# Constant matmuls in TensorE's gaps in the opening of a gated-attention trunk kernel

## Chip, cores and metric

The kernel runs on one core of one Trainium2 chip. The metric is the device time of one execution in microseconds (us). Three runs of the kernel before took 1215.12, 1215.80 and 1216.45 us; the median is 1215.8.

## What is computed

One layer over x, 1024 tokens by 1024 channels, all in float32. Cut to what matters:

```
mod = silu(c) @ ada_w + ada_b
shift, scale, gate = split(mod, 3)
h = rms_norm(x, norm_w) * (1 + scale) + shift
proj = h @ w_in
hq, hf, hi, hz, gq, gk, gv, gz, ga, mg = split(proj)
y_h = hgrn2_branch(hq, hf, hi, hz, lb, hgrn_norm_w)       # gated linear recurrence, 8 heads
y_g = gla_branch(gq, gk, gv, gz, ga, alpha_w, alpha_b, gla_norm_w)   # the same, 4 heads
merged = sigmoid(mg0) * (y_h @ w_branch[0]) + sigmoid(mg1) * (y_g @ w_branch[1])
x = x + gate * (merged @ w_out)
out = rms_norm(x, final_norm_w)
```

The change lies in the opening, where `h` is made and its first products with `w_in` (the columns of `gq` and `gk`) are formed.

## The kernel before

A large product is done as three float32r products: each operand is split into a high part (a cast on ScalarE, line 196) and a low part (a subtraction on VectorE, line 197), and high by high, high by low and low by high are summed in PSUM (`product`, line 350). Smaller products are plain float32 matmuls, each of which TensorE runs as two instructions.

The opening works on the first 512 tokens ("half" 0), four tiles of 128 tokens each, and on channels in blocks of 128. Its steps, in the order in which they are written:

- **Loads.** `load_x` (line 138) brings four tiles of x, `load_mod` (line 243) the columns of `ada_w` for shift and scale of one block of channels, `load_wg` (line 310) rows of `w_in`. All are issued by SyncE (SP), in the order of lines 143 to 144 and 360 to 367; later ones behind line 419.
- **Token norm.** `square_x` (ScalarE, line 200) and `scale_x` (VectorE, line 207) normalise one tile of x. `vec_rows` (line 152) turns a few rows of parameters into columns by a TensorE transposition; the one at line 371 handles `ada_b` and `norm_w`.
- **Transposition.** `turn_x` (line 214) transposes one block of 128 channels of the four tiles on TensorE into PSUM, line 219; `copy_x` (line 223) copies the result to SBUF on ScalarE. `transpose_x` (line 226) does both.
- **Modulation of one block.** `blocks` (line 240) lists five blocks of one or two times 128 channels. The contraction over 1024 has eight parts: `add_mod` (line 259) sums four of them on VectorE, `mm_mod` (line 271) does the other four by matmuls at line 277 with 32 columns each, and `end_mod` (line 280) adds the two (line 283), sums over the partitions by matmuls against a column of ones (line 287) and forms shift and scale (lines 290 and 292).
- **h and its products.** `make_h` (line 230) applies scale and shift on ScalarE (line 233) and splits the result. `products` (line 355) does one, two or three of the three parts of the product for all six accumulators: four in `acc0` (tiles `pd`) and two in `sc_ps`. `sc_ps` is a PSUM tile of 128x1024 that is first written by these products; its second half, columns 512 to 1023, is the sixth accumulator.

For the first block the order is: transposition of channel block 0, `add_mod(0)`, `mm_mod(0)`, `end_mod(0)`, `prep_wg(0)`. Then in the loop at line 378, with `bi` 0: `make_h`, preparation of two blocks of weights, `add_mod(1)`, transpositions of the next two blocks, the first part of the products, `mm_mod(1)`, the second part, `end_mod(1)`, the third part.

The order of the work on TensorE, ScalarE and VectorE is the written one from line 159 (`manual_schedule`) to line 446 (`order.close()`). Outside of it, and for SyncE and GpSimd throughout, the program's builder orders the instructions by when it reckons them ready and by the order in which they are written. Behind line 446 follow the rest of the products, the scans of the two branches, and the merging and output products (lines 541, 1343 and 1520 on TensorE).

`ones` (line 118) and `ident` (line 116) are constant 128x128 float32 tiles in SBUF, all ones and the identity, made by GpSimd at the start.

## Time and profile before

| | before |
|---|---|
| median of three runs | 1215.8 us |
| the profiled execution's own time | 1216.46 us |
| its span, first to last instruction | 1214.8 us |
| TensorE busy (matmuls) | 1184.1 us, 97% of the span |
| VectorE busy | 790.9 us, 65% |
| ScalarE busy | 546.9 us, 45% |
| GpSimd busy | 123.8 us, 10% |
| moved by DMA | 183.51 MB, 151 GB/s on average |

In the rows of the profile PE is TensorE's matmul side, PEld its weight loads, DVE is VectorE, ACT is ScalarE, POOL is GpSimd and SP is SyncE; SPq is SP's queue, from which transfers are issued. `L219` is line 219 of the kernel. In a row of the timeline the first number is the start in us from the beginning of the span, the second the duration, and `x4` says that four instructions of one kind were merged into the row; in brackets stands how long the engine had been idle and what ended it. The strip of 40 digits on the page gives the busy tenths in 40 equal slices of the span, about 30 us each. PEclk is the clock that was granted to TensorE.

### The profile page before, as it was taken

How to read it: one execution, taken by the hardware profiler on the slowest of the kernel's cores; microseconds unless marked ns; L12 is line 12 of the kernel's file. 1: busy time of each engine (PE TensorE's matmuls, PEld its weight loads, DVE VectorE, ACT ScalarE, POOL GpSimd, SP SyncE). 2: the span in 40 equal slices, each digit the busy share in tenths (PEclk: the TensorE clock that was granted, in tenths of full speed). 3: DMA queues.
4: the chain of work that ended last, by engine and by line, in shares of the span. 5: the costliest groups of instructions: out<-in, count | busy, mean ns of one | idle time of the engine just before them, and what ended most of it. 6: DMA issues, size and time to landing. Idle time of an engine off the chain costs nothing.

```text
span 1214.8 us, 20860 instructions
## 1 busy us (share of the span) xinstructions
PE 1184.1 (97%) x8579; PEld 982.6 (81%) x8579; DVE 790.9 (65%) x1245; ACT 546.9 (45%) x797; POOL 123.8 (10%) x215
## 2 busy tenths in 40 slices
PE   5999999999999999999999999999999999999997
PEld 3777889889798888888887888877778888878886
DVE  4637444774848456877884365794653775988994
ACT  5646732434434244344332324455743544444554
POOL 4100000202111121121110101011220000000000
PEclk9999999999999999999999999999999999999999
DMA  9814000844444267255341112054697746435523
GB/s 320 277 70 139 18 19 19 293 141 161 156 152 149 66 207 249 94 179 169 108 174 47 59 53 70 36 174 158 227 343 277 260 160 208 135 104 173 174 104 122
DMA packets 130961, 183.51 MB, mean 151 GB/s; under 512 B 7467, under 2 KB 97633, under 8 KB 130866
## 3 DMA queue, kind: packets, MB, share of 16 engines
q1 hardware_dynamic: 117250, 136.87, 35.7%
q0 software_dynamic: 13568, 45.31, 9.6%
q8 instruction: 67, 1.10, 0.4%
q14 instruction: 28, 0.23, 0.1%
q10 hardware_dynamic: 48, 0.01, 0.0%
HBM read 132.87 MB, written 49.28 MB: 150 GB/s over the span
## 4 chain that ended last, share of the span: by engine, by line
PE 61%; issue 23%; DVE 3%; ACT 3%; POOL 2%; DMA 1%; POOLq 0%; ACTq 0%; DVEq 0%
PE pd L541 19%; PE pd L1343 9%; PE sc_ps L1343 5%; PE pm L1343 5%; PE pd L1520 3%; PE pd L643 2%; PE pd L644 2%; PE pd L645 2%; PE sc_ps L1520 2%; PE pm L848 1%; PE pd L352 1%; PE pm L829 1%; PE pm L850 1%; PE pm L1520 1%; PE sc_ps L352 1%
## 5 line engine op out<-in xcount | busy, mean ns | idle before, releaser
L541 PE MATMUL pd<-b,b 128*128 128x512 f32 x1632 | 387.4, 394 | 0.0
L541 PEld LDWEIGHTS pd<-b,b 128*128 128x128 f32 x1632 | 302.4, 188 | 64.8 <-issue 1.4
L1343 PE MATMUL pd<-b,b 128*128 128x512 f32 x720 | 173.7, 392 | 4.3 <-ACT b L1414 2.1
L1343 PEld LDWEIGHTS pd<-b,b 128*128 128x128 f32 x720 | 133.7, 188 | 35.7 <-ACT b L1414 3.2
L197 DVE TENSOR_TENSOR b<-b,b 128x1024 fp32r<-128x1024 f32 (+2 forms) x89 | 98.9, 1122 | 83.1 <-ACT b L196 65.4
L196 ACT CAST b<-b 128x1024 fp32r<-128x1024 f32 (+2 forms) x89 | 82.9, 948 | 92.1 <-DVE b L1199 14.6
L1286 DVE TENSOR_TENSOR b<-b,b 128x1024 fp32r<-128x1024 f32 x56 | 68.3, 1224 | 66.9 <-ACT b L1285 52.3
L1285 ACT CAST b<-b 128x1024 fp32r<-128x1024 f32 x56 | 58.3, 1050 | 73.9 <-PE pd L1343 20.6
L1343 PE MATMUL sc_ps<-b,b 128*128 128x512 f32 x324 | 79.4, 391 | 1.0 <-ACT scT L793 1.0
L600 PE MATMUL pd<-b,b 128*128 128x256 f32 x256 | 74.2, 290 | 0.0
L1264 DVE TENSOR_TENSOR b<-b,b 128x1024 fp32r<-128x1024 f32 x48 | 59.2, 1251 | 20.8 <-ACT b L1263 15.1
L602 PE MATMUL pd<-b,b 128*128 128x256 f32 x256 | 72.5, 283 | 0.0
L601 PE MATMUL pd<-b,b 128*128 128x256 f32 x256 | 72.4, 283 | 0.0
L1343 PEld LDWEIGHTS sc_ps<-b,b 128*128 128x128 f32 x324 | 60.3, 188 | 14.6 <-ACT scT L793 1.4
L1343 PE MATMUL pm<-b,b 128*128 128x512 f32 x300 | 72.1, 389 | 0.0
L1263 ACT CAST b<-b 128x1024 fp32r<-128x1024 f32 x48 | 49.9, 1050 | 41.2 <-PE pd L1343 16.0
L1343 PEld LDWEIGHTS pm<-b,b 128*128 128x128 f32 x300 | 56.3, 188 | 11.7
L352 PE MATMUL pd<-b,b 128*128 128x512 f32 x192 | 53.3, 410 | 2.0 <-ACT b L196 0.9
L1201 POOL DMA_DIRECT2D ws<-b x64 | 34.6, 541 | 192.0 <-DVE b L1195 86.5
L735 ACT COPY xb<-b 128x512 f32<-128x512 f32 x48 | 29.4, 620 | 49.4 <-PE sc_ps L715 26.7
L643 PE MATMUL pd<-b,b 128*128 128x512 f32 x128 | 51.3, 401 | 0.0
L644 PE MATMUL pd<-b,b 128*128 128x512 f32 x128 | 50.0, 390 | 0.0
(285 smaller groups left out, 1964.3 us busy)
## 6 DMA issues: line engine op xcount, KB each, us to landing
b<-in_w_in_dram SPq DMA_DIRECT2D x66, 512.0 KB, 4.2
ws<-b POOLq DMA_DIRECT2D x64, 256.0 KB, 3.3
b<-ws SPq DMA_DIRECT2D x32, 512.0 KB, 4.9
b<-in_x_dram SPq DMA_DIRECT2D x16, 512.0 KB, 5.7
b<-in_ada_w_dram SPq DMA_DIRECT2D x32, 256.0 KB, 6.9
b<-in_w_branch_dram SPq DMA_DIRECT2D x16, 512.0 KB, 4.4
b<-h SPq DMA_DIRECT2D x14, 512.0 KB, 4.3
wo<-b POOLq DMA_DIRECT2D x14, 512.0 KB, 5.7
```

Of the source, the lines that this page charges most:

```text
L196: nc.scalar.copy(hi, src)
L197: nc.vector.tensor_sub(lo, src, hi.bitcast(F32))
L352: nc.tensor.matmul(accs[f], wg(a, d, f), b[d][:, half * 512:half * 512 + 512], start=(d == 0 and n == 0), stop=(d == KT - 1 and n == 2))
L541: nc.tensor.matmul(ps[0:w, th * 512:(th + 1) * 512], a[:, k, 0:w], b[:, th * 512:(th + 1) * 512], start=(k == 0 and n == 0), stop=(k == KT ...
L600: nc.tensor.matmul(o, lh, hi[:, k % 4, :], start=(k == 0), stop=False)
L601: nc.tensor.matmul(o, lh, lo[:, k % 4, :], start=False, stop=False)
L602: nc.tensor.matmul(o, ll, hi[:, k % 4, :], start=False, stop=(k == KT - 1))
L643: nc.tensor.matmul(o, lh, hi[:, k % 2, :], start=(k == 0), stop=False)
L644: nc.tensor.matmul(o, lh, lo[:, k % 2, :], start=False, stop=False)
L1286: nc.vector.tensor_sub(lo, t, hi.bitcast(F32))
L1343: nc.tensor.matmul(o, a[:, sl], c, start=(p in (1, 5) and kt == 0 and n == 0), stop=(kt == 3 and n == 2), skip_group_check=True)
L1520: nc.tensor.matmul(o, a, b, start=(p in (1, 5) and kt == 0 and n == 0), stop=(kt == 3 and n == 2), skip_group_check=True)
```

## The change

Seventeen calls of a float32 matmul of 128x128 by 128x128 on the constant tiles `ones` and `ident` are added on TensorE; their result goes to columns 512 to 639 of `sc_ps` and is overwritten by the first product of the sixth accumulator. Three stand behind the transposition of the parameter rows, two, four, three and two behind the four transpositions of channel block 0, one behind `mm_mod(0)`, and two between the transpositions of the next blocks and the first products. Line 372's `transpose_x` is written out as its two steps.

```diff
+    def keep_busy(n):
+        for _ in range(n):
+            nc.tensor.matmul(sc_ps[:, 512:640], ones, ident, start=True, stop=True)
+
-    def turn_x(half, xs, d):
+    def turn_x(half, xs, d, gaps=(0, 0, 0, 0)):
         if d % 2 == 0:
             hT[half, d // 2] = S.get([2, 512])
         turned[half, d] = mtile()
         for i in range(4):
             nc.tensor.transpose(turned[half, d][:, i * P:(i + 1) * P], xs[i][:, d * P:(d + 1) * P], ident)
+            keep_busy(gaps[i])
...
     vec_rows(rows_a, 24, R_SH)
-    transpose_x(0, x_t, 0)
+    keep_busy(3)
+    turn_x(0, x_t, 0, (2, 4, 3, 2))
+    copy_x(0, 0)
     add_mod(0)
     mm_mod(0)
+    keep_busy(1)
     end_mod(0)
     prep_wg(0)
...
         if nd == 1:
             for d in nxt:
                 transpose_x(0, x_t, d)
+            keep_busy(2)
             products(d0, (0,))
             mm_mod(bi + 1)
             products(d0, (1,))
```

`if nd == 1` holds in the loop for `bi` 0 alone, since the loop is left before it for the last block.

## The prediction

> **What bounds the kernel now.** I read the page first, then busy time by stretches, then the order of time of the opening.

> ```profile
> span 1214.8 us, 20860 instructions
> ...
> PE   5999999999999999999999999999999999999997
> ...
> PEclk9999999999999999999999999999999999999999
> DMA  9814000844444267255341112054697746435523
> ```

> TensorE (PE) is full in every slice but the first and the last. So the kernel's length is the time at which the products begin, plus a nearly fixed queue of products. The stretches say this more exactly (us; busy time and count of PE, PEld, DVE, ACT, POOL; granted clock; DMA share; GB/s):

> ```profile
> 0.00:24.45 24.45, 11.17 (x40) 5.88 (x40) 13.18 (x30) 14.10 (x27) 14.41 (x56) 1.00 0.96 311
> 24.45:1207.00 1182.55, 1172.98 (x8541) 976.70 (x8539) 775.47 (x1212) 530.56 (x766) 109.41 (x159) 1.00 0.45 148
> ...
> 8.00:14.00 6.00, 1.42 (x3) 0.54 (x3) 3.35 (x9) 3.26 (x7) 5.76 (x22) 1.00 1.13 305
> 14.00:23.00 9.00, 7.71 (x30) 4.62 (x30) 6.41 (x15) 5.19 (x11) 1.30 (x5) 1.00 1.07 366
> 23.00:32.00 9.00, 8.53 (x46) 6.05 (x48) 4.28 (x8) 4.53 (x8) 0.59 (x1) 1.00 1.08 362
> ```

> From 24.45 to 1207 us PE is busy for 1172.98 of 1182.55 us. Only 9.57 us are open there, and the change edits nothing in them. In the opening PE is idle for more than half of the time, while the DMA engines are full (share 1.07 to 1.13). The stretch of the first 24 us is therefore where the change must win or lose, and DMA is the first suspect for its bound. In order of time (start, duration, line, count, idle before and what ended it):

> ```profile
> 3.08 0.27 PE L154 MATMUL pm<-ident,rows_a 24*128 24x24 f32 x1 [0.49 <-DMA rows_a<-in_norm_w_dram]
> 7.34 0.48 PE L219 MATMUL pm<-ident,b 128*128 128x128 f32 x1 [3.99 <-DVE b L210]
> 8.69 0.47 PE L219 MATMUL pm<-ident,b 128*128 128x128 f32 x1 [0.88 <-DVE b L210]
> 11.43 0.47 PE L219 MATMUL pm<-ident,b 128*128 128x128 f32 x1 [2.27 <-DVE b L210]
> 13.11 0.47 PE L219 MATMUL pm<-ident,b 128*128 128x128 f32 x1 [1.21 <-DVE b L210]
> 14.47 1.08 PE L277 MATMUL pm<-b,cs 128*32 128x256 f32 x8 [0.88 <-DVE scT L267]
> 16.17 0.99 PE L287 MATMUL pm<-ones,scT 128*128 128x1 f32 x4 [0.62 <-DVE scT L283]
> 17.02 1.95 PE L219 MATMUL pm<-ident,b 128*128 128x128 f32 x8
> 19.17 2.07 PE L352 MATMUL pd<-b,b 128*128 128x512 f32 x4 [0.20 <-ACT b L196]
> 21.04 1.05 PE L352 MATMUL sc_ps<-b,b 128*128 128x512 f32 x2
> 22.02 1.05 PE L277 MATMUL pm<-b,cs 128*32 128x512 f32 x4
> 23.47 1.05 PE L277 MATMUL pm<-b,cs 128*32 128x512 f32 x4 [0.39 <-DMA b<-in_ada_w_dram]
> 24.45 1.21 PE L352 MATMUL pd<-b,b 128*128 128x512 f32 x4
> ```

> Two things are to be seen. First, at 23.47 the second half of the second modulation step (mm_mod(1)) starts when its weights land, after 0.39 us of waiting. From there PE runs on without a gap into the products at 24.45. Second, PE runs at half speed up to 22.02 (the halves of mm_mod(1) on either side of the wait already take the same 1.05), as the same work later in the kernel shows:

> ```profile
> 28.92 1.20 PE L352 MATMUL pd<-b,b 128*128 128x512 f32 x4
> 29.95 0.62 PE L352 MATMUL sc_ps<-b,b 128*128 128x512 f32 x2
> 30.41 1.07 PE L352 MATMUL pd<-b,b 128*128 128x512 f32 x4
> ...
> 55.34 0.64 PE L277 MATMUL pm<-b,cs 128*32 128x256 f32 x8
> ...
> 58.77 0.50 PE L287 MATMUL pm<-ones,scT 128*128 128x1 f32 x4
> ...
> 63.33 1.04 PE L219 MATMUL pm<-ident,b 128*128 128x128 f32 x8
> ```

> Six products take 22.02 - 19.17 = 2.85 us at the start and 30.41 - 28.92 = 1.49 us later. Eight transpositions take 1.95 against 1.04 us. The clock row reads full in the slow stretch too, so there I trust the durations and not the clock row.

> **The change part by part.** It removes nothing, moves nothing and adds no wait or DMA. It adds 17 calls of a 128x128 float32 matmul on constant tiles.

> *Price of one.* The nearest row at full speed has the same shape:

> ```profile
> L829 PE MATMUL pm<-b,b 128*128 128x128 f32 x112 | 14.0, 277 | 0.4 <-ACT b L808 0.4
> ```

> A float32 matmul is two instructions (mm_mod(0) issues four calls and shows x8). That gives 2 x 14.0 / 112 = 0.25 us at full speed. At half speed the nearest row is the eight transpositions of the same shape, one instruction each: 2 x 1.95 / 8 = 0.49 us. I take 0.49 where the clock is not yet up, and 0.25 as the other end.

> *Where they lie, at 0.49.* The three after the transposition at 3.08 end at 3.35 + 1.47 = 4.82; the next work starts at 7.34, so they are hidden. The two after the first x transposition end at 7.82 + 0.98 = 8.80 against 8.69, 0.11 late, which is hidden since the fourth transposition sets what follows. The four end at 9.27 + 1.96 = 11.23 against 11.43: hidden. The three end at 11.90 + 1.47 = 13.37 against 13.11: the fourth transposition is 0.26 late. The next two then end at 13.84 + 0.98 = 14.82 against 14.47, so mm_mod(0) is 0.35 late. The one behind it ends 0.49 after mm_mod(0), within the 0.62 us in which PE waits for DVE: hidden. The last two follow the eight transpositions. With the 0.35 these end at 19.32, so the two end at 20.30 against 19.17, and the first products are 1.13 late. At 0.25 each, every group fits its gap; the last two fit because the eight transpositions, started 0.93 earlier (below), then end at 16.09 + 1.04 = 17.13.

> *What full speed saves, if it comes before mm_mod(0).* mm_mod(0) takes 0.64 for 1.08 (0.44 saved) and the four at L287 take 0.50 for 0.99 (0.49 saved). These two are on the chain to the first products: the sums from L287 give the scale, ACT then scales and casts, and PE starts:

> ```profile
> 17.65 0.82 ACT L233 ACTIVATE b<-b,modv,amul 128x512 f32<-128x512 f32 x1 [1.38 <-DVE amul L292]
> 18.50 0.62 ACT L196 CAST b<-b 128x512 fp32r<-128x512 f32 x1
> ```

> So the products start at 19.17 - 0.93 = 18.24. They take 1.49 for 2.85 and end at 19.73 for 22.02. That is 2.29 us won on PE.

> *Where the 2.29 us go.* The next instruction that cannot move is the second half of mm_mod(1). Its data come by the queue of SP, which issues it in this order:

> ```profile
> 11.40 6.31 SPq L251 DMA_DIRECT2D b<-in_ada_w_dram x8
> 18.10 1.09 SPq L315 DMA_DIRECT2D b<-in_w_in_dram  x2
> 19.60 6.14 SPq L251 DMA_DIRECT2D b<-in_ada_w_dram x8
> ```

> The eight transfers of block 1 are issued from 11.40 to 17.71 us into full DMA engines, each behind a landing of an earlier transfer, and none behind PE. A faster PE does not move them. PE then waits 0.39 + 2.29 = 2.68 us before 23.47 in place of 0.39. What is late next is the landing, and it was late before. The other branch to the same point is DVE:

> ```profile
> 24.58 0.69 DVE L283 TENSOR_TENSOR scT<-scT,pm 128x512 f32<-128x512 f32 x1
> 25.96 0.95 PE L287 MATMUL pm<-ones,scT 128*128 128x1 f32 x8
> ```

> DVE's sum at 24.58 needs the end of mm_mod(1) at 24.52, which stays. It ends at 25.27 and PE asks for it at 25.96, behind its products. So nothing after 23.47 is pulled forward.

> *Sum.* Gain 0, since the landing covers all of the 2.29 us. In the other direction, if the clock stays low throughout, the products end 1.13 us later, at 23.15. The first half of mm_mod(1) then takes 1.05 and ends at 24.20, against 23.47, so 0.7 us are lost. I take 0, since PE is occupied almost without a hole from 11 us on and reached full speed before after 19.17 to 22.02 of dense work. Bounds from this sum are 0 and +0.7 us on the profiled execution's 1216.46 us (span 1214.8 and 1.7 around it), which stands 0.66 above the median of 1215.8.

> [...] The clock row shows nothing of the switch, but the durations put it at 22.02. [...]

> **The rivals.**

> *The clock's moment varies between executions.* If the switch came after 23.47 in some of the runs before, these lost time on path. The rows bound it: the three runs spread from 1215.12 to 1216.45, 1.33 us, and median to lowest is 0.7. An early switch would bring all runs to the lowest: about 1215.1. Against it stands that the profiled execution had the switch in time and yet took 1216.46. [...]

> *The landing is not the bound.* Were the wait at 23.47 for something on PE's or DVE's side, the 2.29 us would come through: 1215.8 - 2.3 = 1213.5. For it: the wait is only 0.39 us, so without it PE's speed would decide at once. Against it: the row names the transfer, and the DMA engines are full.

> *The added matmuls stand in the way at half speed* (the change does not do what it says): 1215.8 + 0.7 = 1216.5, decided by whether the products after the last two start later than 19.17.

> *Slower: the order behind the opening is laid anew.* From line 446 on, the builder of the program, and not the source, orders the instructions of PE, ACT and DVE by its own reckoning of when each is ready. The added calls shift that reckoning. The place is the later stages, where PE waits now and then:

> ```profile
> PE pd L1343 <- ACT b L1414: 2.1, 2, 1.8
> PE pd L1343 <- DVE b L953: 1.5, 1, 1.5
> ```

> An order that repeats these three waits elsewhere costs 3.6 us: 1219.4. It decides from the first place after 65 us at which two instructions have changed places. For it: 9.57 us of gaps exist, so gaps can grow or shrink. Against it: all three engines follow PE, so a common shift leaves most orders alone. A luckier order could give as much back: 1212.2.

> **How the numbers follow.** Hidden behind the landing, 0.52: about 1215.5, the median less a share of the second case. The clock's moment, 0.13: 1215.1. The landing not the bound, 0.05: 1213.5. Added matmuls in the way, 0.10: 1216.5. New order, 0.20: 0.12 slower, 0.08 faster. What a measurement of this kernel can tell from no change is about 0.2%, 2.4 us; even the full 2.29 us stay just under it. Faster by more is the lucky order and most of the third case, where noise helps it over: 0.12. Slower by more is the new order and 0.04 out of the first case for something that these rows do not show: 0.16. Within: 0.72. The range takes in the bounds, the 1213.5 case, and goes most of the way to the two ends of the new order: 1212.8 to 1218.8. The likeliest case's own range is 1214.5 to 1216.8.

> **What would show it.** Right: six products in about 1.5 us from about 18.3, then a wait of 2 us or more for the transfer before mm_mod(1), and its second half still at about 23.4; equal times from there to the end. Wrong: the second half of mm_mod(1) clearly before 23.4 (landing not the bound); transpositions at 1.95 us for eight and products after 19.5 (in the way); an order on PE that differs after line 446 and gaps beyond 9.57 us (new order). A transfer landing at another time without the queue having changed would break the central step.

## The result, and the profile after

The changed kernel takes 1219.69 us (median of 8 runs, 1218.78 to 1221.96) against 1215.93 us for the kernel before in the same job (8 runs, 1214.74 to 1217.61). The medians differ by 3.8 us, 0.31%; the ratio worked out from all 16 runs is 1.0034 with a 95% interval of 1.0024 to 1.0043. The kernel is slower, where no change was forecast. One execution of e1 below, the one that was profiled, took 3040.09 us with all its products slow, and is left out of the figures.

The page of the profiled execution (1220.52 us by its own time) has, beside the lines shown of before:

```profile
span 1218.8 us, 20928 instructions
...
PE   7999999999999999999999999999999999999997
...
PEclk9999999999999999999999999999989999999999
...
q8 instruction: 67, 1.10, 0.4%
```

The first slice is busier, as the added matmuls make it. There are 68 more instructions. And the clock row has a dent in the thirtieth slice, 884 to 914 us, which the kernel before did not have. The same stretches as before (columns as there):

```profile
0.00:24.45 24.45, 15.49 (x74) 11.08 (x74) 13.22 (x30) 13.99 (x27) 14.55 (x56) 1.00 0.95 308
24.45:1207.00 1182.55, 1172.15 (x8525) 975.98 (x8524) 773.12 (x1204) 528.50 (x760) 109.37 (x159) 1.00 0.45 147
```

PE is as full behind the opening as it was, but gets through 16 matmuls fewer (x8525 for x8541). Where time is lost cannot be seen from busy time here: a matmul at half clock counts as busy for longer (12 products take 5.49 us in place of 3.02 in the rows further down). TensorE's timeline in the opening:

```profile
14.79 1.08 PE L282 MATMUL pm<-b,cs 128*32 128x256 f32 x8 [0.38 <-DMA b<-in_ada_w_dram]
15.80 0.71 PE L216 MATMUL sc_ps<-ident,ones 128*128 128x128 f32 x2
16.49 0.58 PE L292 MATMUL pm<-ones,scT 128*128 128x1 f32 x4
...
19.07 1.21 PE L357 MATMUL pd<-b,b 128*128 128x512 f32 x4 [0.63 <-ACT b L196]
20.12 0.62 PE L357 MATMUL sc_ps<-b,b 128*128 128x512 f32 x2
22.27 1.05 PE L282 MATMUL pm<-b,cs 128*32 128x512 f32 x4 [1.52 <-DMA b<-in_ada_w_dram]
23.77 1.05 PE L282 MATMUL pm<-b,cs 128*32 128x512 f32 x4 [0.44 <-DMA b<-in_ada_w_dram]
24.75 1.20 PE L357 MATMUL pd<-b,b 128*128 128x512 f32 x4
```

The clock record of this execution starts at 16.28 us; up to there the durations are those of half speed, behind it of full speed (before: 22.02). The six first products take 20.74 - 19.07 = 1.67 us for 2.85. Then PE waits 1.52 and 0.44 us for `ada_w`, and the products behind go on at 24.75, 0.30 later than before. So the opening gives nothing and loses little. The order of instructions, but for the added calls, is that of before on all five engines. I set the starts of the same PE instructions side by side: the changed kernel is 0.3 us late at 24.45, 0.7 from 313 on, 0.2 at 886 (it gains a little between 830 and 860), 1.3 at 893, 4.2 at 900 and 4.0 at the end.

Most of the loss thus lies in 7 us around 893, where the output product begins. First the kernel before (L1414 is the sigmoid of `put_gate1` on ScalarE, L1415 its store by GpSimd), then the kernel after, whose lines there are 9 higher:

```profile
887.31 0.54 POOL L1415 DMA_DIRECT2D gate<-b  x1 [3.01 <-ACT b L1414]
...
892.22 0.60 ACT L1414 ACTIVATE b<-pd 128x512 f32<-128x512 f32 x1 [0.76 <-DMA gate<-b]
...
892.87 3.02 PE L1343 MATMUL pd<-b,b 128*128 128x512 f32 x12 [1.82 <-ACT b L1414]
```

```profile
887.98 0.54 POOL L1424 DMA_DIRECT2D gate<-b  x1 [3.49 <-ACT b L1423]
...
893.49 0.60 ACT L1423 ACTIVATE b<-pd 128x512 f32<-128x512 f32 x1 [1.97 <-DMA gate<-b]
...
894.14 5.49 PE L1352 MATMUL pd<-b,b 128*128 128x512 f32 x12 [2.88 <-ACT b L1423]
```

Read from the last row back: PE wants the PSUM tile that the sigmoid empties; the sigmoid wants the SBUF buffer from which an earlier gate store is still being read; that store was issued at 887.98. From its issue to the sigmoid 5.51 us pass, against 4.91 before. PE waits 2.88 us instead of 1.82: 0.60 of the 1.06 more is this longer store; the rest is that the store was issued 0.67 later, for a reason not followed up, while PE itself came 0.22 later. Then the same 12 products take 5.49 us instead of 3.02. The windows on either side of 893.50 say why:

```profile
890.09:893.50 3.41, 1.17 (x6) 0.63 (x4) 3.12 (x3) 1.44 (x4) 1.61 (x3) 1.00 1.05 398
893.50:900.33 6.83, 6.19 (x15) 4.84 (x16) 0.02 (x1) 1.68 (x3) 0.54 (x1) 0.50 1.00 367
```

The granted clock is 0.50 from 893.50 for 6.83 us. And the store takes longer, it seems, because of a transfer that no line of the source issues. The DMA view over that place, before (887 to 894 us) and after (887 to 895); columns are packets, MB and share of 16 engines:

```profile
q0 software_dynamic: 497, 1.78, 62.6%
q1 hardware_dynamic: 1416, 0.85, 42.9%
```

```profile
q0 software_dynamic: 567, 2.00, 63.0%
q1 hardware_dynamic: 1517, 1.11, 41.9%
q8 instruction: 1, 0.02, 0.9%
```

Queue q8 brought instructions, 67 times 16,384 bytes in an execution of the kernel before. Its page counts 17,158 instructions of TensorE (8579 on PE and as many on PEld), 256 to each of the 67; so I take q8 for TensorE's, an estimate that the runs below bear out. 0.9% of 16 engines over 8 us is 1.15 us of one engine. By the start times of its packets in the trace, a fetch came before at 863.4 and the next at 897.4 us; after, at 859.2 and 890.8, into the store that the boundary waits for. In f4, 256 added instructions brought one fetch more (68 for 67) and put the later ones back to about where they were (863.0 and 895.8 us).

### The profile page after: what moved, and what is told of

It reads as the page before. It is cut to its first block, busy times and chain, and to the rows that moved or that the text cites. A ratio compares the mean times of both kernels' runs of the same rounds, so it can differ in the third digit from the quotient of the medians.

```text
span 1218.8 us, 20928 instructions
## 1 busy us (share of the span) xinstructions
PE 1191.5 (98%) x8613; PEld 989.9 (81%) x8613; DVE 790.8 (65%) x1245; ACT 547.2 (45%) x797; POOL 123.9 (10%) x215
## 4 chain that ended last, share of the span: by engine, by line
PE 64%; issue 19%; DVE 5%; POOL 3%; DMA 2%; ACT 2%; POOLq 0%; ACTq 0%; DVEq 0%
PE pd L550 18%; PE pd L1352 10%; PE sc_ps L1352 5%; PE pm L1352 5%; PE pd L1529 3%; PE pd L652 2%; PE pd L654 2%; PE pd L653 2%; PE pd L611 2%; PE pd L610 2%; PE pd L609 2%; PE sc_ps L1529 2%; PE pm L857 1%; PE pm L838 1%; PE pd L357 1%
## 5 line engine op out<-in xcount | busy, mean ns | idle before, releaser
L196 ACT CAST b<-b 128x1024 fp32r<-128x1024 f32 (+2 forms) x89 | 83.0, 948 | 92.9 <-DVE b L1208 14.4
L1295 DVE TENSOR_TENSOR b<-b,b 128x1024 fp32r<-128x1024 f32 x56 | 68.3, 1224 | 71.3 <-ACT b L1294 49.3
```

The source lines that it names most:

```text
L196: nc.scalar.copy(hi, src)
L1295: nc.vector.tensor_sub(lo, t, hi.bitcast(F32))
```

## The experiments

The theories: **F**, the 68 added instructions shift every later instruction fetch, some now fall into transfers that are awaited, and a longer wait can drop the clock; **A**, each added instruction costs its issue; **H**, the faster opening leaves a hole in front of `mm_mod(1)`, and the clock pays for it; **W**, the early rise of the clock shifts the steps of 3.41 us at which the clock changes, which gives the fall at 893 (in the profile after, 893.50 is 877.22 us, 257 steps of 3.413, behind the rise at 16.28; in f1 to f4 the letter stands for another rival, named there); **N**, chance in when transfers land. That the order was laid anew was out already, since no two instructions had changed places. In e1, e3, e7, e8, e9, f2 and f4 small matmuls are put into the kernel before, one call of which is four instructions of TensorE (two matmuls and two weight loads); what they write is overwritten. They stand in the idle time behind the `vec_rows` call of line 371, so that the clock comes up as late as in the kernel before (21.6 to 23.4 us in the profiles, 19.7 in e3).

```diff
+    def tiny(n):
+        for j in range(n):
+            p0 = j % 4 * 32
+            nc.tensor.matmul(sc_ps[p0:p0 + 32, 512:513], ones[:, 0:32], ident[:, 0:1], start=True, stop=True)
...
     vec_rows(rows_a, 24, R_SH)
+    tiny(17)
```

The number is 17 in e1, e7 and f2 (68 instructions), 32 in e3 (128), 48 in e9 (192), 64 in e8 and f4 (256). e2 and f3 are the changed kernel with `keep_busy(3)` replaced by `tiny(50)`: the early clock, with 256 instructions added. All times are medians in us; each job has its own runs of the kernel before. The ratios are worked out from the runs of both kernels and are not those of the two medians.

| run | added instructions | clock | time | ratio to before, 95% |
|---|---|---|---|---|
| after, f1 | 68 | early | 1219.69, 1218.92 | 1.0034 [1.0024, 1.0043], 1.0034 [1.0019, 1.0049] |
| e1, e7, f2 | 68 | late | 1217.85, 1218.27, 1218.30 | 1.0019 [1.0008, 1.0031], 1.0025 [1.0015, 1.0034], 1.0020 [1.0011, 1.0029] |
| e3 | 128 | late | 1224.82 | 1.0079 [1.0056, 1.0103] |
| e9 | 192 | late | 1219.35 | 1.0028 [1.0016, 1.0041] |
| e2, f3 | 256 | early | 1216.90, 1217.25 | 1.0009 [0.9999, 1.0019], 1.0010 [1.0001, 1.0020] |
| e8, f4 | 256 | late | 1216.93, 1216.50 | 1.0010 [1.0000, 1.0019], 1.0007 [0.9995, 1.0020] |
| e4 | 68, other buffers | early | 1224.53 | 1.0068 [1.0046, 1.0089] |
| e6 | 256, hole filled | early | 1217.12 | 1.0010 [1.0000, 1.0020] |

**e1, the instructions without the early clock.**

> The kernel before plus 68 TensorE instructions that do almost no work (17 calls of 32 columns by 1), all in the hole between 3.4 and 7.3 us; no early clock. The result of these calls is overwritten. Theory F (instruction fetch): the changed kernel has the same orders on all engines, but its 68 more TensorE instructions move the fetch of the next 16 KB of instructions from 897 to 891 us, into the gate store that TensorE waits for at the boundary of the first two gate stages; the wait grows from 1.8 to 2.9 us and the clock falls to half for 6.8 us. It expects a fetch at 890 to 892 us, a clock drop near 893 us and 1219 to 1221 us. Theory W (early clock): the early switch of the clock at 16 us shifts the windows in which the clock is decided; without it there is no drop: 1215 to 1217 us. Theory N (chance in the landing of transfers): no drop or a drop without relation to the fetch, runs spread over 1215 to 1221 us.

Measured 1217.85, 1.9 above the kernel before: under F's range and above W's. About half of the loss is there without any early clock. e7 repeats the kernel for a profile.

**e2, the early clock with the fetches put back.**

> The changed kernel with its first three calls replaced by 50 small ones (32 columns by 1), so that TensorE has 256 instructions more than before, one whole fetch; the other 14 calls and so the early clock stay. Theory F: fetches fall near 863 and 897 us as in the kernel before, no drop at 893: 1215 to 1217 us. Theory W: early clock as in the changed kernel, so a drop near 893 and 1219 to 1221 us. Theory N: as for the first.

Measured 1216.90. With 188 instructions more than the changed kernel it is 2.8 us faster than that was in its own job. In its profile the fetch stands at 897.3 us, as before, and the clock does not fall at 893. That is what F named, and against W. The clock rises at 20.66 there, hardly earlier than before; in f3, the same kernel, at 12.05.

**e3, half of a fetch.**

> The kernel before plus 128 TensorE instructions (32 small calls) in the same hole, half a fetch. Theory F: the fetch near the boundary falls at about 883 to 886 us, where the loads before the boundary run and not the gate store; the wait stays near 2 us and there is no drop: 1215 to 1217 us. Theory W: 1215 to 1217 us as well. Theory N: spread.

A miss for F's number: 1224.82, the slowest of the row, without any fall of the clock in its profile. The fetches of this count hit other places. TensorE's waits, before and then e3 (total, times, longest):

```profile
PE pd L352 <- DVE b L331: 0.8, 1, 0.8
PE sc_ps L715 <- DVE tot L718: 0.7, 1, 0.7
```

```profile
PE sc_ps L721 <- DVE tot L724: 2.3, 3, 1.7
...
PE pd L357 <- DVE b L336: 1.9, 1, 1.9
```

The wait in the opening's products at 109 us is 1.1 longer, with a fetch at 94.1 in the loads of `w_in` before it, and three waits for the scan's sums (L715 in the kernel before) stand where one stood, with fetches at 232.6, 299.5 and 338.1. That these fetches cause these waits is argued from their times alone, and the waits named make 2.7 of the 5.9 us by which TensorE is late in this profile. F does not say in advance which waits a count will hit; what it says is that the cost goes up and down with the count, not along with it.

**e4, the changed kernel with the wait at the boundary taken away.** The unsummed odd outputs of `put_gate1` get slices of the tile `xb_f` in place of a shared buffer:

```diff
     def put_gate1(d, half, ap, summed):
-        g = ap if summed else Q.get()
+        own = d % 2 == 1 and not summed
+        g = xb_f[:, d // 2 * 512:d // 2 * 512 + 512] if own else ap if summed else Q.get()
...
-        Q.free(g)
+        if not own:
+            Q.free(g)
```

> The changed kernel, but the four gate outputs that TensorE's banks wait for at the boundary are written to four buffers of their own, so that ScalarE need not wait for an earlier gate store to land. Nothing else differs but some places in the order of ScalarE, GpSimd and SyncE around it. All theories that put the loss into this wait (F and N) expect TensorE's wait at 891 us to fall under 1.5 us and no clock drop: 1214 to 1216.5 us. If the clock falls for another reason (W by windows alone), the drop stays: 1218 to 1221 us.

A miss: 1224.53. The wait did not go, it grew:

```profile
895.03 1.04 ACT L1294 CAST b<-b 128x1024 fp32r<-128x1024 f32 x1 [3.24 <-DMA b<-in_w_in_dram]
896.98 1.04 ACT L1294 CAST b<-b 128x1024 fp32r<-128x1024 f32 x1 [0.90 <-DMA gate<-b]
```

```profile
899.09 3.36 PE L1352 MATMUL pd<-b,b 128*128 128x512 f32 x7 [4.21 <-ACT xb L1424]
```

The sigmoid does not need the gate buffer any more, but stands behind two casts on ScalarE that wait for landings of `w_in` and of the same store. The edit has also changed the order of ScalarE, GpSimd and SyncE at this place, a fetch at 893.7 lies in the wait, and the clock fell behind it, at 896.85 for 6.83 us. So removing the wait itself was not achieved, and this run says nothing of what the boundary would take without it. It shows something else, in the opening:

```profile
21.99 1.05 PE L282 MATMUL pm<-b,cs 128*32 128x512 f32 x4 [1.98 <-DMA b<-in_ada_w_dram]
23.48 1.92 PE L282 MATMUL pm<-b,cs 128*32 128x512 f32 x4 [0.44 <-DMA b<-in_ada_w_dram]
```

The second half of `mm_mod(1)` takes 1.92 us for 1.05: the clock, up since 12.80, fell at 23.04 for 3.41 us, behind a hole of 1.98 us. That was the ground for H.

**e6, the hole filled.** e2 with eight calls of `tiny` fewer and eight matmuls between the first products and `mm_mod(1)`; they add zeros to the sixth accumulator, so that its value stays:

```diff
             products(d0, (0,))
+            for _ in range(8):
+                nc.tensor.matmul(sc_ps[:, 512:640], ones, cs32[:, :, 1:17], start=False, stop=False)
             mm_mod(bi + 1)
```

> As e2 (early clock, 256 TensorE instructions more than before), but eight of the small calls are replaced by eight float32 matmuls that add zeros to the sixth accumulator, between the first products and mm_mod(1), where the changed kernel's TensorE waits for 1.5 us. Theory H (the hole): the early clock opens this hole, and in some executions the clock falls back to half at about 23 us for one window; e2's runs lost 4.25 us each to a clock under full, the kernel before 2.8. Filled, the loss falls to 2.8 or less and the time to 1214.5 to 1216. If the hole is not the cause: as e2, 1216.9, with a loss of 4 us.

Measured 1217.12, against 1216.90 and 1217.25 without the filling. The clock did not fall in its profile, and the mean time lost to a lower clock went from 4.2 us in e2 to 3.2 (H: 2.8 or less), but the time is not better. H names something that happens, and at this count it costs nothing that shows; with 68 instructions the filling was not tried.

**e7, e8, e9: the count alone.**

> The kernel of the first experiment once more (68 small instructions, no early clock), since its profiled execution ran at a low clock from end to end. Theory F: 1218 to 1220 us; in the profile a fetch of instructions at 890 to 892 us and TensorE's wait before 893 us longer than 2.4 us. Theory N: any wait, without relation to the fetch.

> The kernel before plus 256 small TensorE instructions (64 calls) in the first hole, one whole fetch, no early clock. Theory F: all later fetches fall where they fell before, so 1215 to 1217 us. Theory A (every added instruction costs by itself, 0.04 to 0.07 us as the runs with 68 and 128 would have it): more than 1225 us.

> The kernel before plus 192 small TensorE instructions (48 calls), three quarters of a fetch, no early clock. Theory F: the fetches fall some 20 us before their old places in the dense stages (near 91, 231, 298, 327 and 874 us); those at 231 and 298 fall into loads that VectorE and ScalarE wait for, so 1217 to 1222 us, with TensorE's longer waits each behind a fetch. Theory A: about 1224 us.

68 instructions cost 2.7 us in this job (1218.27 against 1215.61), 256 cost 1.3. That takes A out: nearly four times the instructions cost less. e9 is slower by 3.7 through other places: its profile has nothing at the boundary, but the wait for the scan's sum at 313 is 2.13 us, with a fetch at 292.5.

```profile
313.46 0.89 PE L715 MATMUL sc_ps<-xb,b 128*32 128x48 f32 x64 [0.66 <-DVE tot L718]
```

```profile
314.19 0.89 PE L724 MATMUL sc_ps<-xb,b 128*32 128x48 f32 x64 [1.22 <-DVE tot L727]
```

```profile
316.23 0.89 PE L721 MATMUL sc_ps<-xb,b 128*32 128x48 f32 x64 [2.13 <-DVE tot L724]
```

These are the kernel before, the one after, and e9, at the same place. That is also where the changed kernel's 0.5 us at 313 come from. This wait follows the count through all profiles: 0.66 us before, 0.17 to 0.40 with 256 (e2, e6, e8, f3, f4), 1.22 to 1.75 with 68 (after, f1, e7, f2), 1.71 in e3 and 2.13 in e9, with early clock and with late.

**f1 to f4: clock and count crossed in one job.** f1 is the changed kernel again, f2 is e1, f3 is e2, f4 is e8.

> The changed kernel once more, so that early clock and count of instructions stand crossed in one job (early clock, 68 added). Theory F (68 added instructions shift the instruction fetches into awaited transfers, and the early clock costs a little more by itself through the wait it opens before the second half of mm_mod(1)): 1219.0 to 1220.0 us, 0.8 to 1.5 above the run with 68 small instructions and no early clock. Rival W (the early clock costs nothing; its surplus in earlier jobs was the chip's difference): within 0.5 us of that run.

> The kernel before with 17 small matmuls (68 instructions) and no early clock. F and W: 1218.2 to 1218.8 us, 2.3 to 2.9 above the kernel before. If the added instructions' place in the stream is not what costs: 1215.5 to 1216.2.

> The changed kernel with 256 added instructions (early clock, fetches back at the points of before). F: 1216.5 to 1217.2 us. If the early clock costs by itself at this count too, 0.5 us or more above the run with 256 and no early clock; if it gains, 0.5 or more below; W: equal within 0.4.

> The kernel before with 64 small matmuls (256 instructions) and no early clock. F: 1216.5 to 1217.2 us, 0.8 to 1.3 above the kernel before for a reason still open. If that surplus was the chip's of the earlier job: 1215.5 to 1216.1.

Against 1216.21 for the kernel before (32 runs): 1218.92, 1218.30, 1217.25, 1216.50. The place in the stream is confirmed: 68 instead of 256 instructions cost 1.7 us with the early clock and 1.8 without; by resampling the 9 to 12 runs of each, 0.4 to 5.0 and 0.0 to 2.8, and e7 against e8 in their job gives 1.3 (0.7 to 2.6). The early clock adds 0.6 and 0.75 us; these two differences reach from -0.4 to 3.7 and from -0.9 to 1.8, so this job does not tell them from nothing, and F's 0.8 to 1.5 is neither met nor excluded. The early clock saves nothing at either count. The surplus at 256 shrank to 0.3 here and cannot be told from zero.

**The boundary in all profiles that have it in the same form.** The second column is from the issue of the gate store to the start of the sigmoid that waits for it; the third is PE's busy time in the 3.41 us ahead of the fall of the clock, or in the one of these windows that holds most of the wait (they are counted from the profile's first rise of the clock).

| profile | store to sigmoid, us | PE busy of 3.41 | half clock behind it, us | fetch inside |
|---|---|---|---|---|
| before | 4.91 | 2.05 | none | no |
| e2, e6, e8 (256) | 4.58, 4.91, 4.15 | 2.22, 1.70, 1.89 | none | no |
| f3, f4 (256) | 4.76, 4.52 | 2.43, 1.63 | none | no |
| e9 (192) | 4.84 | 1.64 | none | no |
| e3 (128) | 4.08 | 1.71 | none | no |
| after, f1 (68) | 5.51, 5.47 | 1.17, 0.51 | 6.83, 3.41 | yes |
| e7, f2 (68) | 5.63, 5.67 | 1.26, 1.02 | 3.41, 3.41 | yes |

Without a fetch the store takes 4.08 to 4.91 us and PE waits 1.52 to 1.93, with one 5.47 to 5.67 and 2.39 to 3.06; and all four profiles with a fetch fall to half clock there, with early clock or late, none of the eight others does. That speaks against W and N. The two sides of it, f2 and then f4, which differ by the number of small matmuls alone (a DMA row of f2 between the two timeline rows, from 887 to 895 us; f4's view of 887 to 894 us has no row of q8):

```profile
886.90 0.54 POOL L1421 DMA_DIRECT2D gate<-b  x1 [2.85 <-ACT b L1420]
```

```profile
q8 instruction: 1, 0.02, 0.8%
```

```profile
893.22 4.61 PE L1349 MATMUL pd<-b,b 128*128 128x512 f32 x12 [2.39 <-ACT b L1420]
```

```profile
887.02 0.54 POOL L1421 DMA_DIRECT2D gate<-b  x1 [3.38 <-ACT b L1420]
...
892.19 3.01 PE L1349 MATMUL pd<-b,b 128*128 128x512 f32 x12 [1.78 <-ACT b L1420]
```

That the fetch itself, and not something else that comes with this count, holds up the store was not tried on its own: no run moved a single fetch and left the others.

## Why the prediction was wrong

*The bound of the opening* was right. The wait is for the landing of `ada_w`, and a faster PE waits for it. f1 runs nearly the course that was worked out:

```profile
18.20 1.20 PE L357 MATMUL pd<-b,b 128*128 128x512 f32 x4 [0.63 <-ACT b L196]
19.23 0.62 PE L357 MATMUL sc_ps<-b,b 128*128 128x512 f32 x2
21.83 1.05 PE L282 MATMUL pm<-b,cs 128*32 128x512 f32 x4 [1.97 <-DMA b<-in_ada_w_dram]
23.32 1.05 PE L282 MATMUL pm<-b,cs 128*32 128x512 f32 x4 [0.45 <-DMA b<-in_ada_w_dram]
```

Products at 18.20 (18.24 predicted), a wait of 1.97 + 0.45 = 2.42 us in two pieces (2.68 in one), the second half of `mm_mod(1)` at 23.32 (23.47). Only the split was missed: the first half, too, waits for its own transfer.

*The price and the hiding* of the added matmuls were right. At half speed the first six instructions take 1.65 us, 0.55 a call, and at full speed four take 0.61, 0.30 a call (0.49 and 0.25 predicted). The case that they stand in the way did not come: the clock was up by 16.28 and in f1 by 11.28, against 22.02 before.

*The clock's moment* in the kernel before cost nothing that could be seen to be won: with the same count of 256, the early clock is not faster (1216.90 and 1216.93, in two jobs; 1217.25 and 1216.50 in one).

*The step that failed* is the one that closed the account at 24.45 us: "Only 9.57 us are open there, and the change edits nothing in them", and with it the "nearly fixed queue of products"; from this came the bounds of 0 and +0.7 and, as the only named way to more, an order laid anew. The order stayed. But the change does edit what lies behind: 68 instructions move the later boundaries of 256 in TensorE's stream, and with them fetches: from 863.4 to 859.2 and from 897.4 to 890.8 us in the two profiles. In the profile of the changed kernel TensorE lost 0.5 us at the scan's sum at 313, 1.1 us at the gate store (0.6 of it the store's own longer time), and 2.9 us through the clock that fell behind the longer wait, from 893 to 900. Both halves of it could be seen beforehand: q8 with 67 packets on the page, and the wait of 1.8 us at the boundary in the row that the prediction shows. The slower rival named the right place, the wait of L1343 for L1414, and its 1219.4 was near the 1219.69; its mechanism was refuted, so that is no credit to it.

*How the 3.8 us divide.* 68 instructions with the late clock cost 1.9 to 2.7 us (ratios 1.0019, 1.0025, 1.0020). In the profiles of e7 and f2 this lies at the boundary: TensorE is 0.4 and 0.2 us ahead of the kernel before at 890 us, and 1.8 and 1.9 behind at 898. The rest of the 3.8, some 1 to 2, comes with the early clock, and its cause stays open. In the profiles it is one more window of 3.41 us at half clock: the fall at the boundary lasts 6.83 us in the changed kernel, for 3.41 in e7 and f2, and f1 has a second fall at 315. These are two profiles, and one job alone (f1 against f2, 0.6) does not resolve the difference. The mean time lost to a lower clock (span by one minus the mean granted clock) does not settle it: it is 5.3 and 5.0 us in the changed kernel's runs (after, f1), 3.0, 3.8 and 3.8 in e1, e7 and f2, and 2.4 to 2.8 in the kernel before; but it is also 4.2 and 4.3 in e2 and f3 against 2.2 and 2.9 in e8 and f4, where the times do not differ so. Whether 256 added instructions cost the last 0.3 to 1.5 us stays open as well. None of the kernels was faster than the one before.

## What to carry to other kernels

The 68 instructions added to TensorE, busy for 97% of the span here, changed more than their own time: two of its fetches stood 4.2 and 6.6 us earlier against the data transfers (859.2 and 890.8 us for 863.4 and 897.4). So check the instruction queue's fetch times against the waits that end on a DMA. Before crediting or blaming an edit for a few tenths of a per cent, run a control with the same number of harmless instructions and another with a whole fetch's worth (256 here): 68, 128, 192 and 256 cost 2.2, 8.9, 3.7 and 0.8 us here (late-clock runs over the kernel before of their job, means where there are several). And look for waits of some 2 us in a dense TensorE stretch: here a wait of 1.8 us that grew to 2.4 to 3.1 was followed by 3.41 or 6.83 us of half clock as well.

## What the runs showed of the hardware

```profile
18.88:22.29 3.41, 1.42 (x7) 0.75 (x8) 3.34 (x8) 2.05 (x5) 0.00 (x0) 1.00 1.10 357
22.29:25.70 3.41, 3.41 (x9) 0.56 (x6) 1.58 (x3) 0.00 (x0) 0.00 (x0) 0.50 1.06 371
```

  These two windows of f3 are the hole that the early clock itself opens in front of `mm_mod(1)`, and its price: 0.9 us at 24.45. Gaps of 1.98 to 2.88 us stood there ahead of falls (e4 at 23.04, f3, f2, e7, after), in windows that were idle for 58 to 70%; f1's gap of 1.97 us in front of `mm_mod(1)` was not followed by one.
- **Reaching full clock earlier did not hold by itself.** Of the five profiles with the early clock and the hole open (after, e2, e4, f1, f3), two (e4, f3) fell again at 22 to 23 us.
- **The clock row was blind at the start.** In the kernel before it reads 1.00 up to the first record (22.02 us), while eight transpositions take 1.95 us there and 1.04 later.
